# A hybrid decoder trunk: two first weight loads on another queue, later outputs and norms in the differential heads, other places in the tile before the last, roots one group behind, two output jobs begun

## The chip, the cores and the metric

The kernel runs on one core of a Trainium2 chip, as one program. The metric is the device time of one execution in microseconds (us). Before the change the median of three runs is 1193.19 us (1192.76 to 1195.35).

The engines are written as in the profile: PE (TensorE, matmuls), DVE (VectorE), ACT (ScalarE), POOL (GpSimd) and SP (SyncE, which here only issues DMAs). Each has its own queue and takes its instructions in a fixed order.

## The reference

The reference is a two-layer decoder trunk over 512 tokens of width 1024, in float32:

```
h = x
h += W_out [ dilated_mixture(qa, ka, va) | rms(differential(qb, kb, vb)) ]   # q, k, v from one projection of rms(h)
h += W_down( gelu(g) * v ),  [g | v] = conv3( W_up rms(h) )
h += W_out( rg_lru(conv4(xr)) * gelu(gate) ),  [gate | xr] = W_in rms(h)     # layer 1
h += W_down( gelu(g) * v )                                                   # second feed-forward
```

Differential attention takes two softmaxes per head and subtracts lam times the second from the first; its output is normalised once more per head (`b_sub_norm`). The recurrent unit has r = sigmoid(block matmul), i = sigmoid(block matmul), a = exp(-8 r softplus(-a_param)), and scans h = a h + sqrt(1 - a^2) (i x).

## The kernel before, in words

Activations lie transposed, channels on the partitions and the 512 tokens along the free axis. Every matmul of the projections is three products of halves (`mm3`): each float32 operand is split into a high part (`wh`, `xh`) and the remainder (`wl`, `xl`). For a weight unit SP loads the raw block, ACT casts it to `wh` (L104) and DVE subtracts to `wl` (L106); units are fetched two ahead.

**Attention.** Eight tiles run in a row: four differential heads (the B tiles, n = 0 to 3), then four pairs of dilated heads (the A tiles, n = 4 to 7). Each tile has 16 groups of six projection matmuls (L348 to L350, output `pj`). The list `line` holds the 128 groups and, behind them, the first matmuls of the output projection (`early_out`, output `mm`, three matmuls a piece). Everything else of a tile is put between groups of `line` by `place(g, f)`, with `g` from the table that `where(n)` returns, counted in groups from the start of the tile, so that 27.3 falls among the next tile's groups. The table's keys: `qk` the transposes of q and k (`qkt`, L414), `sc` the scores with their softmax in three batches (`S`, L447; 128 and 256 columns, then 384, then 512), `tr` the transposes of the probabilities (`pt`, L468, called pt1 to pt4 here, each followed by the cast `pth` on ACT, L471, and the remainder `ptl` on DVE, L472), `out` the product with v (`O`, L482 to L484), and `norm` for the B tiles (`norm`). PE keeps the order in which the code is written; for ACT and DVE a scheduler fixes the order when the program is built.

In a B tile `out` also copies O to `ob` (L571), squares it to `obsq` (L573) and splits the squares in `obh` (ACT, L126) and `obl` (DVE, L127); `norm` begins with two matmuls that sum them over the partitions (`obms`, L129 with `obh`, L130 with `obl`). The softmax of a row block is one DVE instruction that adds the bias and takes the maximum (L458), an exponential on ACT (L461) and a scaling (L556, or L515 in an A tile).

**The start.** `first_tile` issues, all on SP, the two halves of the first block of x and of the first weight unit in turn (L306, L307), then three more pairs. ACT casts the halves of the weight unit (L323).

**The recurrent layer.** For eight blocks of 128 channels `lru_in` projects and convolves (`us` L704, `cv` L706 on ACT and three taps on DVE, L708) and splits (`xrh` L820, `xrl` L822); `lru_gates` runs the gates' matmuls two blocks later (`pr`, `pi`) and three functions on ACT (L837 to L839). `lru_decay` takes four blocks at a time: four exponentials (L849) and squares, and directly behind them four square roots (L857). Functions of ACT belong to tables; going from one table to another costs an ACT_TABLE_LOAD. `after(f)` chains these parts on ACT in the order of the calls. At the end `gelu` makes `gh` and `gl` (L897, L899), and `out_proj` runs eight jobs of 24 matmuls, each over k = 0 to 7.

Of the kernel before, what the change touches and what calls it, by code (L numbers as in the profile page):

```python
# [12 lines left out]
F32 = mybir.dt.float32  # L13
# [6 lines left out]
P = 128  # L20
S = 512
D = 1024
KC = D // P
# [4 lines left out]
NT = 8  # L28
# [2 lines left out]


BATCHES = ((0, 1), (2,), (3,))
PLACES = dict(qk=9, sc=(12, 14, 16), tr=(18.5, 20.7, 23.5, 25.2), step=1, out=27.3, norm=29)
LAST = dict(qk=7.5, sc=(9.8, 10.5, 11.2), tr=(12.7, 13.4, 14.2, 15), step=0.35, out=16.2, norm=18)

OUT_GROUP = 0.65
# [25 lines left out]
def trunk(  # L63
# [15 lines left out]
    nc = tc.nc  # L79
# [14 lines left out]
    def nm(s):  # L94
        uid[0] += 1
        return f"{s}{uid[0]}"
# [22 lines left out]
    def mm3(out, wh, wl, xh, xl, first, last, order=lambda ins: ins):  # L119
        order(T.matmul(out, wh, xh, start=first, stop=False))  # L120
        order(T.matmul(out, wh, xl, start=False, stop=False))  # L121
        return order(T.matmul(out, wl, xh, start=False, stop=last))  # L122
# [96 lines left out]
    with ExitStack() as actx:  # L219
# [78 lines left out]
        def first_tile():  # L298


            xr = [ap2.tile([P, 13 * P], F32, tag=("pth", "ptl")[u % 2], name=nm("xr"))[:, : 2 * S] for u in range(4)]
            wr = [rawp.tile([P, 2 * CW], F32, tag="raw", name=nm("raw")) for u in range(4)]
            for u in range(4):
                for j in range(2 if u == 0 else 1):
                    cx, cw = (slice(j * S, (j + 1) * S), slice(j * CW, (j + 1) * CW)) if u == 0 else (slice(None),) * 2
                    nc.sync.dma_start(xr[u][:, cx], xT[u][:, cx])  # L306
                    nc.sync.dma_start(wr[u][:, cw], w_att[ORDER[0], u][:, cw])  # L307
            nc.sync.dma_start(pt[:, KC:], par[:, KC:])
            units = []
            for u in range(4):  # L310
                if u:
                    x_split(xr[u], (2 * u, 2 * u + 1))
                    units.append(split(wr[u], 2 * CW))
                    with tc.issue_after(last.ins):
                        x_square(xr[u - 1], (2 * u - 2, 2 * u - 1))
                    continue
                wh = whp.tile([P, 2 * CW], F32R, tag="wh", name=nm("wh"))
                wl = wlp.tile([P, 2 * CW], F32R, tag="wl", name=nm("wl"))
                for j in range(2):
                    cw = slice(j * CW, (j + 1) * CW)  # L320
                    last = x_split(xr[0], (j,))
                    with tc.issue_after(last.ins):
                        last = A.copy(wh[:, cw], wr[0][:, cw])  # L323
                    V.tensor_tensor(wl[:, cw], wr[0][:, cw], wh[:, cw].bitcast(F32), ALU.subtract)
                units.append((wh, wl))
            x_square(xr[3], (6, 7))
            return units
# [94 lines left out]
        oT = {}  # L422

        def where(n):
            return LAST if n == NT - 1 else PLACES

        def head_bias(h):
            bt = ap2.tile([P, S], F32, tag="bias", name=nm("bias"))
# [113 lines left out]
        def attn_b(n):  # L542

            p = ORDER[n]
            st = {}

            def sc(blocks):
                if blocks[0] == 0:
                    st["b"] = head_bias(4 + p)
                rows = products(tiles[n]["qk"], blocks)  # L550
                for i in blocks:
                    for c in range(2):
                        st[i, c] = softmax_row(rows[c, i], i, st["b"])
                        if c == 0:
                            e0, r0 = st[i, 0]
                            A.activation(e0, e0, AF.Copy, scale=r0)  # L556
                        else:
                            (e0, _), (e1, r1) = st[i, 0], st[i, 1]
                            V.tensor_tensor(r1, r1, lam, ALU.mult)
                            V.scalar_tensor_tensor(e0, e1, r1, e0, ALU.mult, ALU.add)  # L560

            def tr(i):
                if i == 0:
                    st["pt"] = pt_tiles()
                transposed(st[i, 0][0], i, *st["pt"])

            def out():
                o_ps = bank("O")
                pv(o_ps, tiles[n]["v"], *st["pt"])
                st["o"] = smp.tile([P, S], F32, tag="sq", name=nm("ob"))  # L570
                A.copy(st["o"], o_ps)  # L571
                sq = smp.tile([P, S], F32, tag="sm3", name=nm("obsq"))
                A.activation(sq, o_ps, AF.Square)  # L573
                hi = smp.tile([P, S], F32R, tag="sq", name=nm("obh"))
                lo = smp.tile([P, S], F32R, tag="t", name=nm("obl"), bufs=1)
                st["ms"] = mean_rows("obms", hi, sq, lo)

            def norm():
                o = st["o"]
                ps, products_of = st["ms"]  # L580
                products_of(pe)
                y = smp.tile([P, S], F32, tag="sm3", name=nm("oby"))
                A.activation(y, ps, AF.Ln, bias=epsb)
                A.activation(y, y, AF.Exp, scale=-0.5)
                t = smp.tile([P, S], F32, tag="sq", name=nm("obt"))
                V.tensor_tensor(t, y, y, ALU.mult)
                V.scalar_tensor_tensor(t, ps, EPS, t, ALU.add, ALU.mult)
                V.tensor_scalar(t, t, -0.5 * (1.0 - LAM_INIT), 1.5 * (1.0 - LAM_INIT), ALU.mult, ALU.add)
                V.tensor_tensor(y, y, t, ALU.mult)
                V.scalar_tensor_tensor(o, o, col(C_BS), y, ALU.mult, ALU.mult)  # L590
                hi, lo = o_tiles(p)
                A.copy(hi, o)
                V.tensor_tensor(lo, o, hi.bitcast(F32), ALU.subtract)

            at = where(n)
            steps = [(g, partial(sc, b)) for g, b in zip(at["sc"], BATCHES)]
            steps += [(g, partial(tr, i)) for i, g in enumerate(at["tr"])]
            return steps + [(at["out"], out), (at["norm"], norm)]


# [111 lines left out]
    def ffn(l, nxt, last):  # L712
# [37 lines left out]
        down(1, a1)  # L750
        down(2, a2)

    def out_proj(xs, resid, nxt, order=range(KC), begun=()):
        for m in range(KC):
            if m < len(begun):
                ps, (wh, wl) = begun[m]
                k = order[-1]
                c = slice(k * P, (k + 1) * P)
                mm3(ps, wh[:, c], wl[:, c], *xs[k], False, True)
            else:  # L760
                ps = job(xs, order)
            V.tensor_tensor(h[m], ps, resid(m), ALU.add)
            norm_chunk(m, nxt)
# [43 lines left out]
    def after(f):  # L807

        with ExitStack() as st:
            if mark[0] is not None:  # L810
                st.enter_context(tc.issue_after(mark[0].ins))
            mark[0] = f()
# [31 lines left out]
    def lru_decay(ns):  # L844

        def decay():
            for n in ns:

                last = A.activation(rr[n], rr[n], AF.Exp, scale=spm8[:, n : n + 1])  # L849
                a2 = tmp.tile([P, S], F32, tag="sq", name=nm("a2"), bufs=2)  # L850
                A.activation(a2, rr[n], AF.Square)
                V.scalar_tensor_tensor(tt[n], a2, 1.0, tt[n], ALU.add, ALU.mult)
            return last

        def root():
            for n in ns:
                last = A.activation(tt[n], tt[n], AF.Sqrt, bias=tinyb)  # L857
            return last

        after(decay)  # L860
        after(root)

    def lru_scan(n):
        V.tensor_tensor(uu[n], uu[n], tt[n], ALU.mult)
        V.tensor_tensor_scan(uu[n], rr[n], uu[n], 0.0, ALU.mult, ALU.add)  # L865

    def gate_in(n):
        ps = job(xs)
        g = gg[n] = actp.tile([P, S], F32, tag=f"ah{n}", name=nm("gate"))
        V.tensor_tensor(g, ps, state["rs"], ALU.mult)  # L870

    ins = []
    for n in range(KC):
        ins.append(lru_in(n))
        if n > 1:
            lru_gates(n - 2, *ins[n - 2])
        if n == KC // 2 + 1:
            lru_decay(range(KC // 2))
        if n > KC // 2 + 1:
            lru_scan(n - KC // 2 - 2)  # L880
    for n in range(2):
        gate_in(n)
        lru_gates(KC - 2 + n, *ins[KC - 2 + n])
        lru_scan(KC // 2 - 2 + n)
    lru_decay(range(KC // 2, KC))
    for n in range(2, KC):
        gate_in(n)
        if n < 6:
            lru_scan(KC // 2 + n - 2)
    hg = []  # L890

    def gelu():
# [8 lines left out]
        return last  # L901

    after(gelu)
    out_proj(hg, lambda m: h[m], C_FFN_G[1])
    ffn(1, None, True)


# [69 lines left out]
```

## Time and profile before

| what | value |
|---|---|
| median of the runs | 1193.19 us (1192.76 to 1195.35) |
| profiled execution, its own time | 1195.96 us |
| its span | 1194.1 us |
| PE busy | 1181.2 us (99%), 5566 matmuls |
| DVE busy | 811.4 us (68%) |
| ACT busy | 585.6 us (49%) |
| SP queue, data moved | 113.24 MB, 29.8% of 16 DMA engines |
| granted TensorE clock | 1.00 |

The span runs from the first to the last recorded instruction; 1.86 us of the execution's own time lie outside it. A row of a timeline gives the start in the span, the busy time, the engine, the line, the operation and the tiles, and in brackets how long the engine had been idle and what it had waited for. ACTq and SPq rows are instructions that issue a DMA.

### The profile page before, as it was taken

To read this page: it belongs to the slowest core of one execution; us is meant where nothing else is said; L and a number is where in the kernel's file an instruction comes from. 1 tells how busy PE (TensorE), PEld (TensorE's weight loads), DVE (VectorE), ACT (ScalarE), POOL (GpSimd) and SP (SyncE) were. 2 spreads that over 40 slices of the span, in tenths; PEclk is the share of its full clock that TensorE was granted. 3 is DMA by queue.
4 is the path that set the end of the run, shared out by engine and by line. 5 is a ranking of instruction groups with operands and counts; after the bars stand their busy time and mean duration, and the time that the engine had idled before them with its cause. 6 is when DMAs were issued, how large, how long until landed. Compare 5 with 4: busy or idle time off the path is not lost.

```text
span 1194.1 us, 14625 instructions
## 1 busy us (share of the span) xinstructions
PE 1181.2 (99%) x5566; PEld 990.6 (83%) x5566; DVE 811.4 (68%) x1327; ACT 585.6 (49%) x951; POOL 0.7 (0%) x6
## 2 busy tenths in 40 slices
PE   8999999999999999999999999999999999999998
PEld 8988888788888888888888878888888888888887
DVE  6977888688777763577436888668777763677431
ACT  6667788765444432344225688454444441444220
POOL 0000000000000000000000000000000000000000
PEclk9999999999999999999999999999999999999999
DMA  7221222062323232323233313323232323333221
GB/s 255 68 79 54 67 67 71 19 211 89 106 89 106 89 106 88 106 89 106 88 106 102 111 36 124 106 89 102 92 101 94 100 94 95 100 95 100 92 85 54
DMA packets 33910, 114.31 MB, mean 96 GB/s; under 512 B 3888, under 2 KB 4656, under 8 KB 33840
## 3 DMA queue, kind: packets, MB, share of 16 engines
q1 hardware_dynamic: 33552, 113.24, 29.8%
q8 instruction: 44, 0.72, 0.3%
q14 instruction: 26, 0.21, 0.1%
q10 hardware_dynamic: 288, 0.14, 0.0%
HBM read 111.27 MB, written 2.10 MB: 95 GB/s over the span
## 4 chain that ended last, share of the span: by engine, by line
PE 83%; ACT 3%; DVE 2%; issue 0%; DVEq 0%
PE mm L120 26%; PE mm L121 26%; PE mm L122 26%; ACT sm L461 1%; PE pj L348 1%; PE pj L350 1%; PE pj L349 1%; PE pt L468 1%; ACT sm L515 1%; PE S L447 0%; PE O L489 0%; DVE u L865 0%; DVE sm L458 0%; PE qkt L414 0%; DVE cv L708 0%
## 5 line engine op out<-in xcount | busy, mean ns | idle before, releaser
L104 ACT CAST wh<-raw 128x1024 fp32r<-128x1024 f32 (+1 forms) x207 | 211.1, 1021 | 285.8 <-PE mm L121 256.8
L122 PE MATMUL mm<-xh,wl 128*128 128x512 f32 x896 | 348.6, 389 | 0.0
L121 PE MATMUL mm<-xl,wh 128*128 128x512 f32 x896 | 348.6, 389 | 0.0
L120 PE MATMUL mm<-xh,wh 128*128 128x512 f32 x896 | 348.6, 389 | 0.0
L106 DVE TENSOR_TENSOR wl<-raw,wh 128x1024 fp32r<-128x1024 f32 (+1 forms) x207 | 244.8, 1184 | 43.0 <-ACT wh L104 39.4
L120 PEld LDWEIGHTS mm<-xh,wh 128*128 128x128 f32 x896 | 168.2, 188 | 35.0
L121 PEld LDWEIGHTS mm<-xl,wh 128*128 128x128 f32 x896 | 168.2, 188 | 35.0
L122 PEld LDWEIGHTS mm<-xh,wl 128*128 128x128 f32 x896 | 168.2, 188 | 34.9
L708 DVE SCALAR_TENSOR_TENSOR cv<-us,pt,cv 128x511 f32<-128x511 f32 (+2 forms) x216 | 160.5, 747 | 3.5
L120 PE MATMUL mm<-fh,wh 128*128 128x512 f32 x384 | 149.4, 389 | 0.0
L121 PE MATMUL mm<-fl,wh 128*128 128x512 f32 x384 | 149.4, 389 | 0.0
L122 PE MATMUL mm<-fh,wl 128*128 128x512 f32 x384 | 149.4, 389 | 0.0
L704 DVE TENSOR_TENSOR us<-mm,rs 128x512 f32<-128x512 f32 x104 | 71.6, 688 | 93.9 <-PE mm L122 93.6
L740 DVE TENSOR_TENSOR h<-mm,h 128x512 f32<-128x512 f32 (+1 forms) x49 | 33.2, 680 | 141.4 <-PE mm L122 141.4
L348 PE MATMUL pj<-wh,xh 128*128 128x384 f32 x256 | 92.7, 362 | 2.5 <-ACT wh L323 2.5
L729 ACT CAST fh<-cv 128x512 fp32r<-128x512 f32 x48 | 29.8, 621 | 126.4 <-DVE cv L726 126.4
L350 PE MATMUL pj<-wl,xh 128*128 128x384 f32 x256 | 87.2, 341 | 0.0
L349 PE MATMUL pj<-wh,xl 128*128 128x384 f32 x256 | 87.2, 341 | 0.0
L706 ACT ACTIVATE cv<-us,pt 128x512 f32<-128x512 f32 x104 | 84.3, 813 | 0.9 <-DVE us L704 0.6
L120 PEld LDWEIGHTS mm<-fh,wh 128*128 128x128 f32 x384 | 72.1, 188 | 15.0
L122 PEld LDWEIGHTS mm<-fh,wl 128*128 128x128 f32 x384 | 72.1, 188 | 15.0
L121 PEld LDWEIGHTS mm<-fl,wh 128*128 128x128 f32 x384 | 72.1, 188 | 14.9
(202 smaller groups left out, 1238.6 us busy)
## 6 DMA issues: line engine op xcount, KB each, us to landing
raw<-in_w_up_dram SPq DMA_DIRECT2D x96, 512.0 KB, 3.5
raw<-in_w_dn_dram SPq DMA_DIRECT2D x48, 512.0 KB, 3.5
raw<-in_w_att_dram SPq DMA_DIRECT2D x31, 384.0 KB, 3.4
raw<-in_w_ri_dram SPq DMA_DIRECT2D x16, 512.0 KB, 3.5
raw<-in_w_ao_dram SPq DMA_DIRECT2D x8, 512.0 KB, 3.6
raw<-in_w_ro_dram SPq DMA_DIRECT2D x8, 512.0 KB, 3.5
raw<-in_xT_dram SPq DMA_DIRECT2D x4, 512.0 KB, 4.4
out_dram<-h SPq DMA_DIRECT2D x7, 256.0 KB, 2.0
```

What stands on the lines that cost most here:

```text
L104: A.copy(hi, src)
L106: V.tensor_tensor(lo, src, hi.bitcast(F32), ALU.subtract)
L120: order(T.matmul(out, wh, xh, start=first, stop=False))
L121: order(T.matmul(out, wh, xl, start=False, stop=False))
L122: return order(T.matmul(out, wl, xh, start=False, stop=last))
L348: pe(T.matmul(o, xs[k][0][:, tb], wh[:, cw], start=k == 0, stop=False))
L349: pe(T.matmul(o, xs[k][1][:, tb], wh[:, cw], start=False, stop=False))
L350: pe(T.matmul(o, xs[k][0][:, tb], wl[:, cw], start=False, stop=k == KC - 1))
L704: V.tensor_tensor(u, ps, state["rs"], ALU.mult)
L706: A.activation(c, u, AF.Identity, scale=col(wcol + (taps - 1) * stride), bias=col(bcol))
L708: V.scalar_tensor_tensor(c[:, d:], u[:, : S - d], col(wcol + (taps - 1 - d) * stride), c[:, d:], ALU.mult, ALU.add)
L740: V.tensor_tensor(h[m][:, t], ps[:, t], h[m][:, t], ALU.add)
```

## The change

Five edits, none of which changes what is computed:

1. The two halves of the first weight unit are issued by ACT instead of SP.
2. The one table of places becomes three. B tiles put `out` and `norm` later (27.3 to 28.3, 29 to 30.2) and pt4 at 25.4 instead of 25.2, which is still behind the same group. Tile n = 6 gets a table of its own.
3. `oby` of the norm takes the buffer `t` instead of `sm3`.
4. The four roots leave `lru_decay` and become `lru_root`, called one block later.
5. `out_proj` of layer 1 begins two jobs over k = 0 to 6 and finishes them with k = 7; the matmuls are the same ones in another order.

```diff
-PLACES = dict(qk=9, sc=(12, 14, 16), tr=(18.5, 20.7, 23.5, 25.2), step=1, out=27.3, norm=29)
+PLACES_B = dict(qk=9, sc=(12, 14, 16), tr=(18.5, 20.7, 23.5, 25.4), out=28.3, norm=30.2)
+PLACES_A = dict(qk=9, sc=(12, 14, 16), tr=(18.5, 20.7, 23.5, 25.2), step=1, out=27.3)
+LAST_BUT_ONE = dict(qk=9, sc=(12, 14, 15.8), tr=(18.2, 20.2, 22.6, 24.4), step=0.9, out=26.4)
...
-                    nc.sync.dma_start(wr[u][:, cw], w_att[ORDER[0], u][:, cw])
+                    (nc.sync if u else A).dma_start(wr[u][:, cw], w_att[ORDER[0], u][:, cw])
...
-            return LAST if n == NT - 1 else PLACES
+            return {NT - 1: LAST, NT - 2: LAST_BUT_ONE}.get(n, PLACES_A if ORDER[n] < 4 else PLACES_B)
...
-                y = smp.tile([P, S], F32, tag="sm3", name=nm("oby"))
+                y = smp.tile([P, S], F32, tag="t", name=nm("oby"), bufs=1)
...
+    def begin(xs):
+
+        wh, wl = next_unit()
+        ps = mm.tile([P, S], F32, tag="mm", name=nm("mm"))
+        for k in range(KC - 1):
+            c = slice(k * P, (k + 1) * P)
+            mm3(ps, wh[:, c], wl[:, c], *xs[k], k == 0, False, tc.keep_in_program_order)
+        return ps, (wh, wl)
...
+        after(decay)
+
+    def lru_root(ns):
+
         def root():
             for n in ns:
                 last = A.activation(tt[n], tt[n], AF.Sqrt, bias=tinyb)
             return last
 
-        after(decay)
         after(root)
...
-        if n == KC // 2 + 1:
-            lru_decay(range(KC // 2))
-        if n > KC // 2 + 1:
-            lru_scan(n - KC // 2 - 2)
+        if n == half + 1:
+            lru_decay(range(half))
+        if n == half + 2:
+            lru_root(range(half))
+        if n > half + 1:
+            lru_scan(n - half - 2)
...
-    out_proj(hg, lambda m: h[m], C_FFN_G[1])
+    out_proj(hg, lambda m: h[m], C_FFN_G[1], begun=[begin(hg) for _ in range(2)])
```

What this makes of the queues is seen in the built program. Line numbers after the change are two higher up to the norm, and more behind it (L849 becomes L860, L857 becomes L872).

At the start, SP's queue before holds the halves of x (`xr_129`) and of the weight unit (`raw_133`) in turn:

```order
L306 DMA xr_129<-in_xT_dram 128x512
L307 DMA raw_133<-in_w_att_dram 128x384
L306 DMA xr_129<-in_xT_dram 128x512
L307 DMA raw_133<-in_w_att_dram 128x384
L306 DMA xr_130<-in_xT_dram 128x1024
L307 DMA raw_134<-in_w_att_dram 128x768
```

After, ACT's queue begins with these rows:

```order
L158 ACT_TABLE_LOAD
L162 DMA pt<-in_par_dram 128x8
L309 DMA raw_133<-in_w_att_dram 128x384 x2
L233 ACTIVATE xh_150<-xr_129,pt 128x512
L325 CAST wh_148<-raw_133 128x384
L233 ACTIVATE xh_156<-xr_129,pt 128x512
L325 CAST wh_148<-raw_133 128x384
L233 ACTIVATE xh_162<-xr_130,pt 128x512
L233 ACTIVATE xh_166<-xr_130,pt 128x512
L106 CAST wh_170<-raw_134 128x768
L242 ACTIVATE xsq_174<-xr_129 128x512
```

The two weight halves stand on ACT behind a small load of parameters, and the square of the first block of x (`xsq_174`) has moved behind the cast of the second weight unit.

In the B tiles, ACT before takes O of one tile (`ob_849`, `obsq_851`, `obh_853`) ahead of the next tile's softmax (`sm_880`, `sm_887`: 128 columns; `sm_895`: 256):

```order
L571 COPY ob_849<-O_836 128x512
L573 ACTIVATE obsq_851<-O_836 128x512
L104 CAST wh_1039<-raw_1037 128x768
L126 CAST obh_853<-obsq_851 128x512
L461 ACTIVATE sm_880,sum_883<-sm_880,mx_881 128x128
L461 ACTIVATE sm_887,sum_890<-sm_887,mx_888 128x128
L366 COPY qkraw_922<-pj_706 128x256
L378 ACTIVATE v_923<-pj_706,rstd 128x128
L556 ACTIVATE sm_880<-sm_880,sum_883 128x128
L461 ACTIVATE sm_895,sum_898<-sm_895,mx_896 128x256
```

After, the same O (`ob_901`, `obsq_903`, `obh_905`) stands behind the softmax of both batches, and `obh` behind a copy of q and k and of v as well:

```order
L106 CAST wh_1039<-raw_1037 128x768
L463 ACTIVATE sm_858,sum_861<-sm_858,mx_859 128x128
L463 ACTIVATE sm_865,sum_868<-sm_865,mx_866 128x128
L558 ACTIVATE sm_858<-sm_858,sum_861 128x128
L463 ACTIVATE sm_873,sum_876<-sm_873,mx_874 128x256
L463 ACTIVATE sm_880,sum_883<-sm_880,mx_881 128x256
L558 ACTIVATE sm_873<-sm_873,sum_876 128x256
L573 COPY ob_901<-O_888 128x512
L575 ACTIVATE obsq_903<-O_888 128x512
L368 COPY qkraw_922<-pj_706 128x256
L380 ACTIVATE v_923<-pj_706,rstd 128x128
L128 CAST obh_905<-obsq_903 128x512
```

On PE the matmuls stand in these places. Before: pt4, 12 group matmuls, O, 6, S of 128 and 256, 6, the norm's two, 6, S of 384, 12, S of 512. After: pt4, 18 group matmuls, S of 128 and 256, O, 12, S of 384, the norm's two, 12, S of 512.

In the recurrent layer, ACT before runs the last exponential of the first four blocks (`r_6393`), the roots (`t_...` with `tinyb`), and then the convolution of block 6 (`cv_6453`) and the gates of block 4 (`r_6470`, `u_6471`):

```order
L849 ACTIVATE r_6393<-r_6393,spm_466 128x512
L857 ACT_TABLE_LOAD
L857 ACTIVATE t_6224<-t_6224,tinyb 128x512
L851 ACTIVATE a_6413<-r_6393 128x512
L857 ACTIVATE t_6281<-t_6281,tinyb 128x512
L857 ACTIVATE t_6338<-t_6338,tinyb 128x512
L857 ACTIVATE t_6395<-t_6395,tinyb 128x512
L706 ACTIVATE cv_6453<-us_6451,pt 128x512
L837 ACT_TABLE_LOAD
L837 ACTIVATE r_6470<-pr_6462,pt 128x512
L838 ACTIVATE u_6471<-pi_6463,pt 128x512
L839 ACTIVATE t_6472<-r_6470,sp_464 128x512
```

After, block 6's convolution (`cv_6449`) and block 4's gates (`r_6466`, `u_6467`) go ahead of the roots, with a table load more:

```order
L860 ACTIVATE r_6393<-r_6393,spm_466 128x512
L708 ACTIVATE cv_6449<-us_6447,pt 128x512
L862 ACTIVATE a_6413<-r_6393 128x512
L848 ACT_TABLE_LOAD
L848 ACTIVATE r_6466<-pr_6458,pt 128x512
L849 ACTIVATE u_6467<-pi_6459,pt 128x512
L831 CAST xrh_6454<-cv_6449 128x512
L850 ACTIVATE t_6468<-r_6466,sp_464 128x512
L872 ACT_TABLE_LOAD
L872 ACTIVATE t_6224<-t_6224,tinyb 128x512
L872 ACTIVATE t_6281<-t_6281,tinyb 128x512
L872 ACTIVATE t_6338<-t_6338,tinyb 128x512
```

The roots now stand behind the split of block 6 (`xrh_6454`), and two table loads stand where one was between the exponentials and the roots.

## Rows read from the trace of the kernel before

**Rows 1.** The page's first part: busy time of each engine, share, instructions.

```profile
PE 1181.2 (99%) x5566; PEld 990.6 (83%) x5566; DVE 811.4 (68%) x1327; ACT 585.6 (49%) x951; POOL 0.7 (0%) x6
```

**Rows 2.** What PE waited for, whole span: us in total, times, longest us.

```profile
PE O L483 <- DVE ptl L472: 2.6, 3, 1.0
...
PE pt L468 <- DVE o L531: 1.1, 2, 0.8
PE pt L468 <- DVE ptl L472: 1.0, 2, 0.8
PE pr L121 <- DVE xrl L822: 0.7, 1, 0.7
```

**Rows 3.** Timeline of 0.7 to 2.6 us: start, us, queue, line, DMA issued.

```profile
0.77 0.39 ACTq L160 DMA_DIRECT2D pt<-in_par_dram  x1
...
2.12 0.43 SPq L307 DMA_DIRECT2D raw<-in_w_att_dram  x1
```

**Rows 4.** Timeline of 5.9 to 14.0 us, first weight unit.

```profile
8.39 0.51 ACT L323 CAST wh<-raw 128x384 fp32r<-128x384 f32 x1 [2.23 <-DMA raw<-in_w_att_dram]
...
8.95 0.69 PE L348 MATMUL pj<-wh,xh 128*128 128x384 f32 x1 [2.32 <-ACT wh L323]
...
11.78 0.96 DVE L106 TENSOR_TENSOR wl<-raw,wh 128x768 fp32r<-128x768 f32 x1
...
12.96 0.52 PE L348 MATMUL pj<-wh,xh 128*128 128x384 f32 x1
...
13.75 0.34 PE L348 MATMUL pj<-wh,xh 128*128 128x384 f32 x1
```

**Rows 5.** Timeline of 84 to 113 us, PE, second B tile.

```profile
88.33 0.50 PE L483 MATMUL O<-ptl,v 128*128 128x512 f32 x1 [0.95 <-DVE ptl L472]
...
89.95 0.27 PE L484 MATMUL O<-pth,v 128*128 128x128 f32 x1
91.27 0.33 PE L447 MATMUL S<-qh,qh 64*128 64x128 f32 x2
...
93.31 0.40 PE L129 MATMUL obms<-obh,ones_r 128*128 128x512 f32 x1
```

**Rows 6.** Timeline of 90 to 97.5 us, ACT and DVE, the same tile.

```profile
91.96 0.63 ACT L126 CAST obh<-obsq 128x512 fp32r<-128x512 f32 x1
...
92.98 0.68 DVE L127 TENSOR_TENSOR obl<-obsq,obh 128x512 fp32r<-128x512 f32 x1
...
93.91 0.40 ACT L461 ACTIVATE sm<-sm,mx 128x128 f32<-128x128 f32 x1 [1.32 <-DVE mx L458]
...
94.69 0.35 ACT L366 COPY qkraw<-pj 128x256 f32<-128x256 f32 x1
...
95.21 0.40 ACT L556 ACTIVATE sm<-sm,sum 128x128 f32<-128x128 f32 x1
...
95.50 0.50 ACT L461 ACTIVATE sm<-sm,mx 128x256 f32<-128x256 f32 x1
```

**Rows 7.** Timeline of 209 to 229 us, tiles n = 6 and 7.

```profile
210.44 0.81 DVE L472 TENSOR_TENSOR ptl<-pt,pth 128x128 fp32r<-128x128 f32 x3
...
215.68 0.33 PE L447 MATMUL S<-qh,qh 64*128 64x128 f32 x2
```

**Rows 8.** Timeline of 699 to 714 us, recurrent layer.

```profile
699.11 0.69 DVE L704 TENSOR_TENSOR us<-mm,rs 128x512 f32<-128x512 f32 x1
...
705.59 0.80 ACT L706 ACTIVATE cv<-us,pt 128x512 f32<-128x512 f32 x1
...
706.41 1.28 ACT L837 ACT_TABLE_LOAD   x1
707.70 0.69 ACT L837 ACTIVATE r<-pr,pt 128x512 f32<-128x512 f32 x1
```

**Rows 9.** Timeline of 757 to 760 us, the last split ahead of the output projection.

```profile
758.55 0.69 DVE L899 TENSOR_TENSOR gl<-u,gh 128x512 fp32r<-128x512 f32 x1 [0.69 <-ACT gh L897]
...
759.39 0.40 PE L121 MATMUL mm<-gl,wh 128*128 128x512 f32 x1
```

More of the change, by code (lines that the diff above doesn't have):

```diff
@@ L758, in out_proj @@
                 c = slice(k * P, (k + 1) * P)
-                mm3(ps, wh[:, c], wl[:, c], *xs[k], False, True)
+                mm3(ps, wh[:, c], wl[:, c], *xs[k], False, True, tc.keep_in_program_order)
             else:
@@ L870, in gate_in @@
         V.tensor_tensor(g, ps, state["rs"], ALU.mult)
+    half = KC // 2
     ins = []
@@ L883, in trunk @@
         lru_gates(KC - 2 + n, *ins[KC - 2 + n])
-        lru_scan(KC // 2 - 2 + n)
-    lru_decay(range(KC // 2, KC))
+        lru_scan(half - 2 + n)
+    lru_decay(range(half, KC))
     for n in range(2, KC):
         gate_in(n)
+        if n == 2:
+            lru_root(range(half, KC))
         if n < 6:
-            lru_scan(KC // 2 + n - 2)
+            lru_scan(half + n - 2)
     hg = []
```

## The prediction

> **What bounds the kernel now.** I read the busy shares first. PE works 1181.2 us of the span of 1194.1 [rows 1], so only what PE executes, or what keeps PE waiting, can move the time. No edit changes a matmul, so the question is PE's waits. The table of PE's waits [rows 2] is the second view: next to the start it has only O waiting for the remainder of the probabilities (three times, 2.6 us), transposes waiting for `ptl` (1.0) and `o` (1.1), and one gate matmul (0.7). A wait costs PE some 0.17 us more than its idle time, because the next matmul would have started before the one ahead ended: O's second matmul begins at 88.33 after 0.95 idle [rows 5] and is 1.1 late. With that, O's three waits are worth 3.1 us, the three short ones in tiles 6 and 7 about 1.8, the one of 0.8 ahead of them 0.9, and the gates' 1.2 with a short one on `xrh`. Timelines are the third view; they show who is late, and why.
>
> The profiled execution took 1195.96 us, 2.77 over the median of the runs. I make the sum against it and put the difference on the median, which supposes that the runs wait in the same places.
>
> **The start.** PE has done the first half unit and then stands idle 2.32 us, until 8.95, since ACT's cast of the second half waited for its load until 8.39 [rows 4]. That load was issued at 2.12 on SP [rows 3] and took 6.3 us. After the change it is ACT's third DMA. ACT's first is issued at 0.77 and holds its queue 0.39 us [rows 3]; two more at that rate put the second half at about 1.6, half a us earlier, and off the queue in which the large blocks follow. If it lands as soon as the rest of the chain allows, PE goes on at about 6.5: at most 2.4 us gained. At least nothing, if it lands as late as before. A second brake is the clock: matmuls of 384 columns last 0.52 us up to 12.96 and 0.34 from 13.75 on [rows 4], PE's lower and upper level of 1.2 and 2.4 GHz in their length, while the column of the granted clock reads 1.00. If the change to the upper level stays at its time, the head start is spent at half speed and about half of it is lost. The next unit is no obstacle: its `wl` is ready at 12.7 [rows 4], and ACT no longer squares x ahead of its cast, which takes 0.5 off. I take -1.8, nearer to the full gain, because the load that comes late is the only late one.
>
> The rule against this is in the Trainium skill, "DMA: Bandwidth & Descriptors", section "Issuing engines are not separate DMA queues": DMAs run on the same 16 engines whoever issues them, and a second issuer saves only the time to initiate. By that rule the start gains about 0.5, and the sum below would be 1.3 higher; no row of this trace has two busy issuers to decide it.
>
> **The B tiles, out and norm one group later.** O now comes after 18 group matmuls and the first scores, 2 us later, and `ptl` is there: its three waits, 3.1 us, go. Two breaks between groups and other matmuls go as well. I put 0.1 to 0.15 to a break, an estimate from groups of six with and without one beside them: 0.2 to 0.3 a tile. The question is what is late next. It is the norm. On ACT `obh` stood ahead of the softmax; now it stands behind both batches of it. Let T be the first score matmul of a tile, 91.27 in rows 5. Its exponential follows 2.64 later, at 93.91 [rows 6], with `obl` (0.60 to the next start) between on DVE; without `obl` there, it starts at T+2.04. An instruction of ACT starts about 0.1 before its predecessor ends: two exponentials of 128 columns with their sums take 0.78 to the copy at 94.69, copy and `v` together 0.52 to 95.21, a scaling 0.29 to 95.50 [rows 6]; an exponential of 256 columns about 0.5, its scaling about 0.4, `ob` and `obsq` about 0.5 each like `obh`. So `ob` starts at 2.04 + 0.78 + 0.29 + 2 x 0.5 + 0.4 = T+4.5, and `obh` at 4.5 + 1.0 + 0.5 = T+6.0, ends at 6.6, and `obl` ends at T+7.3 (0.63 and 0.68, rows 6).
>
> PE is earlier. From T it runs scores and one group in 2.04 (91.27 to 93.31, rows 5), one more group (1.04), O (88.33 to the end of its last matmul, and the one ahead: about 1.95) and the scores of 384 columns (0.75, as many columns as the first two batches): it wants `obh` at T+5.75 and `obl` at T+5.95. It waits for `obl` about 1.4 us in all. Before, `obl` came (92.98 + 0.68) just in time for 93.71. So each of the first three B tiles loses 1.4 and gains the breaks: tile 0, whose O never waited, is 1.1 slower; tiles 1 and 2 come out even (-0.1 each).
>
> In the fourth B tile the next tile is an A tile, and the built order puts more ahead of `obh`: one more scaling of 128 (0.3), one of 256 (0.4), a second copy pair (0.5), a squaring (0.5), and the first exponential of 384 columns (0.6). By the same steps `obh` starts at T+8.3 and `obl` ends at T+9.7: PE waits 3.7. Less O's 0.8 and the breaks this is 2.6 slower. The pause is time for DVE, so the transpose that waited 0.8 (the longest in rows 2; 0.9 lost) in the next tile waits no more. Sum for the B tiles: 1.1 - 0.2 + 2.6 - 0.9 = +2.6. Bounds: if ACT got to `obh` in time everywhere, -3.1 - 0.9 - 1.0 = -5.0; if each walk is 0.5 short, +4.6.
>
> The buffer of `oby` costs nothing: `obl`, which shares it, is read by the matmul that `oby` waits for anyway.
>
> **Tile n = 6.** The projection tail's three waits are worth 1.8. The new table asks for the third pair of transposes three output matmuls (0.7) and a stall earlier. Its wait was for `ptl` of the first transposes, which DVE began at 210.44 [rows 7] behind the scaling of q and k; that chain comes about 0.6 later, as ACT now runs the second exponential of 384 columns and its scaling ahead of the last copies. I get the first score of the last tile at 217.3 in place of 215.68 [rows 7], and, as the softmax chain from there to the second pt2 is 0.6 shorter, +1.0 at its end. Bounds: -1.8 (all three waits gone) and +2.5 (the chain not shortened, another wait for the same ACT).
>
> **Roots.** `us` of block 6 is ready at 699.8, but ACT comes to its `cv` only at 705.59, behind a table load and the four roots [rows 8]; that makes the gate matmul late. After the change `cv` goes ahead of those, 4.3 us earlier (1.28 for the load, four roots and a square at about 0.6), and the wait of 1.2 goes. One table load more is added to ACT, 1.28 with the next function directly behind it [rows 8]. It lies beside PE's work: block 7's split moves 0.6 later, and was done more than a us before PE asked for it, of which 0.4 is left once PE is 1.2 earlier. I take -1.2; bounds -1.2 and +0.5.
>
> The Trainium skill, "ScalarE: Activation LUTs", section "What ACT_TABLE_LOAD costs", speaks against this edit: a switch costs a drain as well, 2.66 us together. With that, two loads ahead of block 7's split would make it 2.8 late, and the sum 2.4 higher; rows 8 have the next function 1.29 after the load's start, so the trace does not agree.
>
> **Begun jobs.** The last `gl` ends at 759.24 and PE reads it at 759.39 [rows 9]: no loss now, hence nothing to gain: 0, between -0.1 and +0.3.
>
> **Sum.** -1.8 + 2.6 + 1.0 - 1.2 + 0 = +0.6: 1196.6 for a profiled execution, 1193.8 for the median.
>
> **Rivals.** (1) The norms find their splits in time: their waits stay under 0.4 each. For it: ACT is busy under half of the span, and its instructions may run ahead where I queued them. Against: its order is fixed, and the softmax ahead of `obh` needs DVE's answers. Then the B tiles give -5.0 + 4 x 0.3 = -3.8, and the sum is -5.8: 1187.4. If tile 6 succeeds too, 1184.6. (2) The start gives only the issue time, all else as forecast: +1.9, 1195.1. For it: bytes ahead of the second half are the same. Against: the late load is one out of many. (3) Slower: the norm's wait is longer than walked. If the cast of the next weight unit, which heads ACT's list ahead of the softmax and waits for PE's last group, and the bias maximum behind it slip by 0.5, every norm waits 0.5 more, +2.0 over four tiles, and with tile 6's upper end (+1.5) the sum is +4.1: 1197.3. It decides from a wait of 1.9 on in the first three tiles. Against: nothing new is queued ahead of that cast.
>
> **How the numbers follow.** Within 0.2% (2.4 us, about what a measurement of this kernel can tell from no change) lies 1190.8 to 1195.6. The forecast has 0.42, with an own range of 1191.5 to 1196; rival 1 has 0.24, rival 2 0.19, rival 3 0.15. Faster: rival 1 and 0.05 from the forecast's lower end, 0.29. Slower: rival 3, and 0.08 from the upper ends of the forecast and of rival 2, 0.23. Same: 0.48. The range for 8 in 10 reaches from rival 1 to rival 3: 1186.5 to 1197.5.
>
> **What would show it.** Each step has its row: PE's idle time ahead of its second weight half under 0.5 us; no wait of O for `ptl`; waits of the norm's matmuls for `obh` or `obl` of about 1.4 three times and 3.7 once; a wait of pt3 for `ptl` of 1 us or more near 210; none of the gates for `xrl`. I am wrong if the norm's waits sum to under 3 us, or if the start still idles 2 us.

## The result and the profile after

| | before | after |
|---|---|---|
| median of runs, us | 1193.63 (4 runs, 1192.76 to 1195.35) | 1200.99 (4 runs, 1199.80 to 1202.75) |
| profiled execution, us | 1195.96 | 1200.73 |
| its span, us | 1194.1 | 1198.6 |

The ratio is 1.0061, 95% interval 1.0044 to 1.0078: 7.4 us slower, outside of the predicted range. Line numbers of after are two higher than before's from the tables of places on, and 11 to 19 higher behind `begin`.

The page of after, its first part: busy time of each engine, share of the span and instructions.

```profile
PE 1181.4 (99%) x5566; PEld 992.9 (83%) x5566; DVE 813.3 (68%) x1327; ACT 588.2 (49%) x952; POOL 0.7 (0%) x6
```

PE works as long as before [rows 1], so the time has gone into its pauses. The view of PE's waits in after, whole span (us in total, times, longest):

```profile
PE obms L131 <- ACT obh L128: 5.2, 4, 3.1
PE pj L350 <- ACT wh L325: 2.6, 2, 1.7
PE pt L470 <- DVE o L533: 1.5, 1, 1.5
...
PE obms L132 <- DVE obl L129: 0.9, 4, 0.2
PE S L449 <- DVE mx L460: 0.6, 1, 0.6
PE pt L470 <- DVE ptl L474: 0.6, 1, 0.6
```

Against [rows 2], O's three waits and the gate's have gone, and the norm's have come, 6.1 us in two rows. I compared the start of the same instruction in the two traces, mark by mark:

| mark on PE | before, us | after, us | lead (-) or lag so far | this stretch |
|---|---|---|---|---|
| first score of tile 0 | 41.69 | 41.30 | -0.39 | -0.39 |
| 512-column scores of tile 4 (behind the fourth norm) | 149.49 | 153.53 | +4.04 | +4.43 |
| first score of tile 5 | 168.71 | 171.65 | +2.94 | -1.10 |
| first norm behind the attention | 267.66 | 272.51 | +4.85 | +1.91 |
| third norm behind the attention (recurrent layer done) | 803.39 | 806.86 | +3.47 | -1.38 |
| end of PE's last matmul | 1190.32 | 1193.79 | +3.47 | 0 |
| end of the span | 1194.07 | 1198.57 | +4.50 | +1.03 |

From the first of these marks on, two traces of the same program agree to 0.1 us (before and after were each traced twice); only the start scatters, by some 2 us (first score of tile 0 at 39.74 to 41.83 in eight traces with before's start, at 40.32 to 42.66 in five with the new one). For the start the medians of runs are therefore used, for all else the traces.

The norm first. Timeline of after, 90 to 96 us, ACT, DVE and PE in the second B tile, whose first score matmul starts at T = 88.68 (start, us, engine, line, operation, idle time before it and its releaser):

```profile
90.68 0.40 ACT L463 ACTIVATE sm<-sm,mx 128x128 f32<-128x128 f32 x1 [1.24 <-DVE mx L460]
...
93.15 0.57 ACT L573 COPY ob<-O 128x512 f32<-128x512 f32 x1
...
94.62 0.61 ACT L128 CAST obh<-obsq 128x512 fp32r<-128x512 f32 x1
95.26 0.69 DVE L129 TENSOR_TENSOR obl<-obsq,obh 128x512 fp32r<-128x512 f32 x1 [0.16 <-ACT obh L128]
95.28 0.49 PE L131 MATMUL obms<-obh,ones_r 128*128 128x512 f32 x1 [0.69 <-ACT obh L128]
...
96.01 0.50 PE L132 MATMUL obms<-obl,ones_r 128*128 128x512 f32 x1 [0.23 <-DVE obl L129]
```

In [rows 6] `obh` stood 1.95 ahead of the tile's first exponential; now it stands 3.94 behind it, and PE idles 0.69 and 0.23. In the fourth B tile the pause is longer, and it has a second price. PE of after, 145 to 154 us:

```profile
145.31 0.34 PE L449 MATMUL S<-ql,qh 64*128 64x384 f32 x2
148.74 0.50 PE L131 MATMUL obms<-obh,ones_r 128*128 128x512 f32 x1 [3.09 <-ACT obh L128]
149.47 0.80 PE L132 MATMUL obms<-obl,ones_r 128*128 128x512 f32 x1 [0.22 <-DVE obl L129]
150.06 0.53 PE L350 MATMUL pj<-wh,xh 128*128 128x384 f32 x1
...
152.92 0.33 PE L350 MATMUL pj<-wh,xh 128*128 128x384 f32 x1
...
153.53 0.50 PE L449 MATMUL S<-qh,qh 64*128 64x512 f32 x2
```

The same in the view by windows (window, length, then busy time of PE, PEld, DVE, ACT, POOL, granted clock, DMA share, GB/s):

```profile
146.00:149.00 3.00, 0.26 (x1) 0.19 (x1) 2.29 (x9) 3.00 (x9) 0.00 (x0) 1.00 0.00 0
149.00:152.00 3.00, 2.78 (x9) 2.44 (x9) 0.50 (x2) 1.99 (x5) 0.00 (x0) 0.58 0.02 5
152.00:155.00 3.00, 3.00 (x16) 2.34 (x15) 1.72 (x4) 2.52 (x7) 0.00 (x0) 0.85 0.00 0
```

Behind the 3.09 us pause the granted clock is 0.58, PE's lower level of 1.2 GHz: matmuls of 384 columns last 0.53 until about 152.9 and 0.33 after that. From the norm's first matmul to the next scores PE takes 4.79 us. In the second B tile, where the granted clock is 1.00 and PE waits as long for `obl` (0.23), the same matmuls take 3.25 (95.28 to 98.53), and behind the third norm 3.24. So the lower clock costs some 1.55 us, beside the pause itself.

### The profile page after: what moved, and what is told of

It is laid out like the page before. It is cut to its first block, busy times and chain, and to the rows that moved or that the text cites. A ratio compares the mean times of both kernels' runs of the same rounds, so it can differ in the third digit from the quotient of the medians.

```text
span 1198.6 us, 14612 instructions
## 1 busy us (share of the span) xinstructions
PE 1181.4 (99%) x5566; PEld 992.9 (83%) x5566; DVE 813.3 (68%) x1327; ACT 588.2 (49%) x952; POOL 0.7 (0%) x6
## 4 chain that ended last, share of the span: by engine, by line
PE 94%; ACT 4%; DVE 1%; DMA 1%; issue 0%; ACTq 0%; DVEq 0%
PE mm L124 26%; PE mm L122 26%; PE mm L123 26%; PE pj L350 4%; PE pj L351 3%; PE pj L352 3%; ACT sm L463 1%; PE pt L470 1%; PE S L449 1%; ACT sm L517 1%; PE qkt L416 1%; DMA raw<-in_w_att_dram 1%; PE O L491 0%; ACT wh L106 0%; DVE wl L108 0%
## 5 line engine op out<-in xcount | busy, mean ns | idle before, releaser
L742 DVE TENSOR_TENSOR h<-mm,h 128x512 f32<-128x512 f32 (+1 forms) x49 | 33.2, 680 | 141.4 <-PE mm L124 141.4
```

The lines of the kernel that those rows point to most:

```text
L742: V.tensor_tensor(h[m][:, t], ps[:, t], h[m][:, t], ALU.add)
```

## The experiments

Medians stand, with the number of runs, against those of the kernel before on the same chip; brackets are 95% intervals of the ratio.

**The start alone** (start_only).

```
-                    nc.sync.dma_start(wr[u][:, cw], w_att[ORDER[0], u][:, cw])
+                    (nc.sync if u else A).dma_start(wr[u][:, cw], w_att[ORDER[0], u][:, cw])
```

> The kernel before with the first edit alone (both halves of the first weight unit issued by ACT). Theory A (the profile's account of the changed kernel is the whole account, and the start is worth what its trace shows): the first stamp of per-token sums comes about 0.4 us earlier than in the kernel before, the second half of the weight unit still lands near 8 us, and the time is within 1 us of before. Theory B (the timed runs of before start better than its one profiled execution, and the edit loses about 2.5 us there): 1.5 to 3 us slower than before.

Measured: 1196.07 (10 runs) against 1194.07 (31), ratio 1.0017 [1.0008, 1.0026]: 2.0 us slower, where I had forecast 1.8 gained, as theory B has it. In the traces the first score of tile 0 comes 0.8 later on average (five with the edit, eight with before's start); the 2.0 is that of the medians. Its start, PE and the DMA queues, 0.7 to 8 us:

```profile
0.73 1.34 SPq L306 DMA_DIRECT2D xr<-in_xT_dram  x3
1.19 0.93 ACTq L307 DMA_DIRECT2D raw<-in_w_att_dram  x2
...
5.40 0.51 ACT L323 CAST wh<-raw 128x384 fp32r<-128x384 f32 x1 [0.54 <-DMA raw<-in_w_att_dram]
5.96 0.69 PE L348 MATMUL pj<-wh,xh 128*128 128x384 f32 x1 [1.10 <-ACT wh L323]
...
7.18 0.51 ACT L323 CAST wh<-raw 128x384 fp32r<-128x384 f32 x1 [0.64 <-DMA raw<-in_w_att_dram]
7.74 0.69 PE L348 MATMUL pj<-wh,xh 128*128 128x384 f32 x1 [0.45 <-ACT wh L323]
```

**The kernel before once more** (before_again), unchanged, for the scatter of its start.

> The kernel before, unchanged, for a second trace. Theory A: the same PE stamps within 0.5 us from the first scores on and an end behind PE of 3.7 to 4.8 us, so that the profiled 1195.96 was an execution at the upper end of the runs. Theory B: the second weight half lands 2 us earlier than in the first trace, and all stamps are 2 us earlier.

Measured: 1194.17 (10), ratio 0.9999. Its start:

```profile
1.65 0.42 SPq L306 DMA_DIRECT2D xr<-in_xT_dram  x1
2.11 0.43 SPq L307 DMA_DIRECT2D raw<-in_w_att_dram  x1
2.59 0.43 SPq L306 DMA_DIRECT2D xr<-in_xT_dram  x1
...
4.60 0.49 ACT L323 CAST wh<-raw 128x384 fp32r<-128x384 f32 x1
...
5.14 0.44 PE L348 MATMUL pj<-wh,xh 128*128 128x384 f32 x1 [0.28 <-ACT wh L323]
...
6.73 0.72 ACT L231 ACTIVATE xh<-xr,pt 128x512 fp32r<-128x512 f32 x1 [1.64 <-DMA xr<-in_xT_dram]
...
7.36 0.49 ACT L323 CAST wh<-raw 128x384 fp32r<-128x384 f32 x1
7.91 0.44 PE L348 MATMUL pj<-wh,xh 128*128 128x384 f32 x1 [1.47 <-ACT wh L323]
```

Neither theory holds whole: from the first scores on this trace is 1.3 us ahead of the first one of before. Here the first weight half is cast at 4.60, in start_only at 5.40: the edit delays it. And the second half, in [rows 4] the late load on which I built, lands 1.2 us earlier, at 7.21 in place of 8.37, and 1.3 ahead of the second block of x (512 KB, issued at 2.59). Nor is it the only late load: ACT waits until 6.73 for the second half of the first x block. With the edit SP has two DMAs less ahead of the second block and issues it at 1.65, and the second weight half landed 0.2 to 1.2 us behind it in each of the five traces with the edit (in start_only at 7.16, the block at 6.79).

**The start edit with the first x block in four pieces** (start_split), so that SP issues the second block at 2.6 again.

```
-                    nc.sync.dma_start(xr[u][:, cx], xT[u][:, cx])
+                    for c0 in (cx.start, cx.start + S // 2) if u == 0 else (None,):
+                        cq = cx if c0 is None else slice(c0, c0 + S // 2)
+                        nc.sync.dma_start(xr[u][:, cq], xT[u][:, cq])
```

> The kernel before with the first edit, and with the two halves of the first block of x issued as four DMAs of 256 columns on SP, so that the second block of x is issued at about 2.6 us as before and not at 1.65. Theory A (the edit loses because the second block, 512 KB, is issued ahead of the second weight half and shares the DMA engines with it): the second half lands at 6.5 us or earlier, PE begins it by 7.1, and the time is that of before within 1 us, 2 us under the edit alone. Rival (a load issued on ACT's queue is slower by itself): it lands behind 7.2 us, and the time stays 1.5 to 2.5 us above before.

Measured: 1193.67 (11) against 1193.88 (27), 0.9999 [0.9990, 1.0008]; the second half lands at 5.95, 1.7 ahead of the block (issued at 2.59). PE begins it at 7.55 and not by 7.1, because ACT comes to its cast only behind the second half of x (6.38). The loss has gone, so the issue by ACT is not what costs; what is left is the earlier block. The later first half is not it: it is cast at 5.43 here too. That the four smaller loads of x do something besides was not tested. A gain is not seen either, with an interval of -1.2 to +1.0 us.

**Out and norm of the B tiles alone** (out_norm_only: the tables and the buffer of `oby`).

```
-PLACES = dict(qk=9, sc=(12, 14, 16), tr=(18.5, 20.7, 23.5, 25.2), step=1, out=27.3, norm=29)
+PLACES_B = dict(qk=9, sc=(12, 14, 16), tr=(18.5, 20.7, 23.5, 25.4), out=28.3, norm=30.2)
+PLACES_A = dict(qk=9, sc=(12, 14, 16), tr=(18.5, 20.7, 23.5, 25.2), step=1, out=27.3)
...
-            return LAST if n == NT - 1 else PLACES
+            return LAST if n == NT - 1 else PLACES_A if ORDER[n] < 4 else PLACES_B
...
-                y = smp.tile([P, S], F32, tag="sm3", name=nm("oby"))
+                y = smp.tile([P, S], F32, tag="t", name=nm("oby"), bufs=1)
```

> The kernel before with out at 28.3 and norm at 30.2 in the B tiles and the other buffer for oby, tile n = 6 and all else as before. Theory A (norm waits, and a lower clock behind the long one): PE waits 1.3 to 1.4 us at each of the first three norms and 3.7 at the fourth, the granted clock falls for some 3.5 us behind the fourth, and the time is 3.3 us above before. Rival (the norm waits only take the place of O's, no clock): +1.7 us.

Measured: 1196.89 (10), 1.0024 [1.0014, 1.0033], +2.8; +3.37 between the marks, with the norm's waits of 5.2 and 0.9 as in after, and a granted clock of 0.57 from 149 to 152. That is theory A.

**After with the norm 1 and 3 places later** (after_norm_31 and after_norm_33).

```
-PLACES_B = dict(qk=9, sc=(12, 14, 16), tr=(18.5, 20.7, 23.5, 25.4), out=28.3, norm=30.2)
+PLACES_B = dict(qk=9, sc=(12, 14, 16), tr=(18.5, 20.7, 23.5, 25.4), out=28.3, norm=31.2)
```

(33.2 in place of 31.2 in the second.)

> The changed kernel with norm at 31.2, one group behind the scores of 384 columns. It parts the fourth tile from the other three. Theory A: the first three norms wait 0.3 us at most; the fourth still waits 3 us or more, as another copy pair comes ahead of its split, and the granted clock falls behind it; 1200.99 less 3 x 1.2 gives 1197 to 1198. Rival (the fall of the clock belongs to the sum of the waits, not to the long one): no fall, 1195 or less.

> The changed kernel with norm at 33.2 in place of 30.2, so that the norm's matmuls stand one group behind the scores of 512 columns; all else as changed. Theory A (the norm's waits and the lower clock behind the fourth make most of the loss): no wait of the norm's matmuls, no fall of the clock near 150, some 8 us faster than the changed kernel, 1192 to 1193.5. Rival (the loss lies in the start and in what comes behind the attention): 3 us faster at most, 1197 or more.

Measured: with 31.2, 1195.81 (10) against 1193.88; with 33.2, 1192.97 (10) against 1194.07, 0.9992 [0.9983, 1.0001]. Relative to before that is +1.9 and -1.1, where after is +7.4. PE's waits for the norm with 31.2:

```profile
PE obms L131 <- ACT obh L128: 2.4, 1, 2.4
```

The first three have gone, the fourth is left, with a granted clock of 0.71 and 0.73 from 146 to 152; I had expected 3 us or more of it, and the time is over 1 us below what I had expected. With 33.2 there is no wait of the norm, the clock stays at 1.00, the B tiles take 3.25 less than in before, and one new wait is next, a transpose for `ptl` (1.6 near 152). So the pauses of the norm are what the B tiles lost, and the later O is worth having once the norm follows late enough.

**The table of tile n = 6 alone** (lbo_only).

```
+LAST_BUT_ONE = dict(qk=9, sc=(12, 14, 15.8), tr=(18.2, 20.2, 22.6, 24.4), step=0.9, out=26.4)
...
-            return LAST if n == NT - 1 else PLACES
+            return {NT - 1: LAST, NT - 2: LAST_BUT_ONE}.get(n, PLACES)
```

> The kernel before with the table of tile n = 6 alone. Theory A (as in the trace of the changed kernel: a wait of the scores of 512 columns for the maximum of those of 384, a longer wait of pt3 and of the second pt2): waits of 0.6, 0.6 and 1.5 us in that order, the first norm behind the attention 1.9 us later by the trace, 1.9 slower. Rival (the waits come from the later arrival of the tile, behind the norm's waits): the three waits of before, within 0.5 us of before.

Measured: 1197.35 (9) against 1193.88 (27), 1.0024 [1.0015, 1.0034], with three runs near 1195.4 and six near 1197.5. The trace is of an execution of the upper group (1197.34). In it the three waits are 0.6, 0.6 and 1.5, as theory A has them, the tile costs 1.8, and the last store lands later (below), by 1.2; the time is 1.6 us above what I had expected. What parts the two groups of runs is not settled.

**Roots alone** (root_only: `lru_root` one block later, without the begun jobs).

```
-    out_proj(hg, lambda m: h[m], C_FFN_G[1], begun=[begin(hg) for _ in range(2)])
+    out_proj(hg, lambda m: h[m], C_FFN_G[1], begun=())
```

(taken from after, with its tables, its start and the buffer of `oby` put back too)

> The kernel before with the roots one block later alone; the output jobs of the recurrent layer run whole, as before. Theory A (the begun jobs are what lets the roots' gain through: the last split of the gelu part comes at a time that PE's head start does not move): the gates' wait of 1.2 us goes, a new wait of 0.7 and 0.5 us at the last k of the first output job takes its place, and the time is within 0.5 us of before. Rival (the roots gain by themselves, as forecast): 1.2 us faster.

Measured: 1194.02 (11) against 1193.84 (15), 1.0006 [0.9997, 1.0014]. The gate's wait has gone, and PE is 1.27 earlier up to 758 us. There it waits for the last split, in PE's timeline of root_only:

```profile
757.66 0.39 PE L122 MATMUL mm<-gh,wl 128*128 128x512 f32 x1
758.54 0.50 PE L120 MATMUL mm<-gh,wh 128*128 128x512 f32 x1 [0.50 <-ACT gh L914]
759.27 0.50 PE L121 MATMUL mm<-gl,wh 128*128 128x512 f32 x1 [0.23 <-DVE gl L916]
```

What was won is given back: at 761.90 PE is level with before (761.91). In [rows 9] that split was just in time; an earlier PE makes it late.

**Combinations**, all with before's start and before's table for tile n = 6: later out and norm at 33.2 with the roots, without the begun jobs; then with them; then with the fourth B tile's norm at 39.2 besides (best, best_begun and best_b39).

> The kernel before with the parts that gain by the traces: out at 28.3 and norm at 33.2 in the B tiles with the other buffer for oby, and the roots one block later; the start, tile n = 6 and the output jobs as before. Theory A (the parts add up: -3.2 for the B tiles, -1.3 for the roots): 4.5 us faster than before, 1189 to 1190.5, no wait of O, of the norms or of the gates. Rival (the wait of a transpose for ptl in the first A tile, 1.8 us in the trace with the norm at 33.2, grows, or the gain of the B tiles belongs to the other start): 2.5 us or less.

> The kernel with out at 28.3, norm at 33.2 and the later roots, to which the two begun output jobs are added. Theory A: the wait of 1.2 us at the last k of the first output job goes, 1.2 us faster than without the begun jobs, 1189.1, 4.8 under before. Rival (the begun jobs cost by themselves, two jobs' results coming late together): no gain over 1190.3.

> The same with the norm of the fourth differential head at 39.2 instead of 33.2, so that DVE makes the remainders of the first transposes of the next tile ahead of the norm's arithmetic. Theory A: the wait of the third transposes for them (1.8 us in the traces with norm at 33.2) falls by 0.6, what two instructions of the norm took ahead of them; 1188.5. Rival (the remainders wait for the scaling of q and k anyway): no change, 1189.1.

Measured: 1190.32 (6) against 1193.88, 0.9967 [0.9955, 0.9978]; 1189.67 (5) against 1193.84, 0.9966 [0.9954, 0.9979]; 1188.52 (5) against 1193.84, 0.9954 [0.9941, 0.9968]. The first gains 3.6 where I had expected 4.5: the gates' wait has gone, but it has the same wait for `gh` and `gl` as root_only (0.5 and 0.2, near 754), and the roots give nothing; with the begun jobs it is gone and 1.35 of the roots is kept. The third is 5.3 us faster than before, the fastest median here. PE's waits in it:

```profile
PE pj L351 <- ACT wh L326: 1.2, 2, 1.0
PE O L494 <- DVE ptl L475: 1.1, 1, 1.1
...
PE pt L471 <- DVE o L534: 1.0, 2, 0.8
PE pt L471 <- DVE ptl L475: 0.2, 1, 0.2
```

The transpose's 1.6 has become a wait of O of 1.1, and from the first score of tile 0 to that of tile 5 the trace takes 0.9 us less than the second's. The difference of the medians to the second (1.2 us) lies inside of their intervals.

**After once more** (after_again), unchanged.

> The changed kernel, unchanged, for a second trace and more runs; it asks where the 1 us lies by which its time stands above the sum of its parts (2.0 for the start, 3.3 for the B tiles, 1.8 for tile n = 6, -1.3 for the roots with the begun jobs: 5.8). Theory A (the last store landed late by chance in the first trace): the second trace ends 3.7 us behind PE, and the median of more runs is nearer to 5.8 above before, 1199.5 to 1200. Theory B (the late last store belongs to this program): it ends 4.7 us behind PE again, and the time stays at 1201.

Measured: 1200.74 (5) against 1192.82 (9), 1.0058 [1.0044, 1.0071]; the same marks from tile 0 on, to 0.1 us. The DMAs issued after 1188 us, in after (queue, KB, us from issue to landing):

```profile
out_dram<-h SPq DMA_DIRECT2D x1, 128.0 KB, 1.7
out_dram<-h ACTq DMA_DIRECT2D x1, 128.0 KB, 2.8
```

In before they take 1.7 and 1.8. In this second profile of after the last store again takes 2.8 us, and the span ends 4.74 behind PE (theory B); in lbo_only it takes 3.0. The two kernels with the norm moved later have the same table for tile 6, and end their span 3.74 and 3.75 behind PE, as before does. So the late store comes back with the program. Why is open.

## Why the prediction was wrong, step by step

The forecast was +0.6; measured are +7.4 and, in the repeat, +7.9 between the medians (+6.9 by the ratio). The parts sum to +6.8: start +2.0, B tiles +3.3, tile 6 +1.9, roots with begun jobs -1.4, last store +1.0. What the medians show beyond that was found in no place of the traces. The largest miss is the start, 3.8 us; each other part missed by 1.0 us or less.

- **The bound** was right: PE's busy time did not move, its waits did.
- **The start** (-1.8, measured +2.0) is the step that failed. That the late load "is the only late one" was read from one execution. In the second trace of before it lands 1.2 us earlier, and in seven traces with the same start 0.6 to 2.0 earlier: I took scatter for a property of the order, and took the gain off a median whose executions, by these traces, have less of that wait. I priced ACT's issue of the load and not what SP issues in the room that it leaves: of a moved DMA the queue that it leaves has to be walked as well. The lower bound of no gain was therefore no bound. PE idles 1.70 us ahead of its second half in after and 2.68 in the repeat, where I forecast under 0.5. In place of the gain the runs showed the second half landing behind SP's 512 KB block, and a loss of 2.0 that goes once that block is issued at 2.59 again. Rival 2 came from the Trainium skill, "DMA: Bandwidth & Descriptors", section "Issuing engines are not separate DMA queues"; its first half, that the loads share their engines whoever issues them, agrees with the second half landing behind SP's block. That the second issuer only saves is not what was measured in start_only, and the half microsecond of rival 2 is too small for start_split to tell from none (-1.2 to +1.0 us).
- **B tiles** (+2.6, measured +3.3: tile 0 +1.0, tiles 1 and 2 -0.25 each, tile 3 +4.0, the transposes' wait -1.1). The walk along ACT held: T+2.04, 4.5, 6.0 and 7.3 for the starts of the exponential, `ob` and `obh` and the end of `obl` became 2.00, 4.47, 5.94 and 7.27 in the rows above. The waits walked as 1.4 and 3.7 were 0.7 and 3.1 for `obh`, 0.2 each for `obl`, and with the matmul that would have started before its predecessor ended, some 1.3 and 3.65. O's waits went. The mis-sized term is the fourth tile, +2.6: it left out that PE resumes at 1.2 GHz, 1.55 us, and measured +4.0. I had read both levels at the start [rows 4] and did not apply them to a pause that I had just forecast.
- **Tile n = 6** (+1.0, measured +1.9; lbo_only +1.8) had the right sign and too small a size. The new rows of PE in after are these:

```profile
204.72 0.49 PE L449 MATMUL S<-qh,qh 64*128 64x512 f32 x1 [0.57 <-DVE mx L460]
...
214.41 0.55 PE L470 MATMUL pt<-ident,sm 128*128 128x128 f32 x3 [0.56 <-DVE ptl L474]
...
232.45 0.44 PE L470 MATMUL pt<-ident,sm 128*128 128x128 f32 x2 [1.47 <-DVE o L533]
```

  The second I had named as 1 us or more; it is 0.56. The first, the largest scores waiting for a maximum of the batch ahead, I had not foreseen, and the last, 1.5 in place of 1.1 in two [rows 2], I had put as a chain 0.6 shorter.
- **Roots and begun jobs** (-1.2 and 0, measured -1.4 together). The total is right by luck, since the split is wrong: root_only gives nothing, the begun jobs alone were not run, and the two together keep the gain. By my own rows `gl` is 0.15 ahead of PE; from this I had the begun jobs gain nothing, and did not carry PE's 1.2 earlier into that step. The Trainium skill, "ScalarE: Activation LUTs", section "What ACT_TABLE_LOAD costs", would have made the added table load 2.66 us. The trace does not agree, and it decides: ACT in after has the next function 1.30 behind the load's start, and the gate's wait gone:

```profile
711.08 1.28 ACT L872 ACT_TABLE_LOAD   x1
712.38 2.56 ACT L872 ACTIVATE t<-t,tinyb 128x512 f32<-128x512 f32 x4
```

- **The last store** (+1.0) stood in no step.
- **The rivals.** Rival 1 did not come: PE idled 0.9 us at each of the first three norms and 3.3 at the fourth, not under 0.4. Rival 3 named the right side, with the norm's wait as mechanism; but the waits were the walked ones, not 0.5 longer, and its price of 1197.3 is 3.7 short. It took the start's gain of 1.8 for certain.

## What to carry to other kernels

When a DMA is moved to another queue, walk the queue that it leaves too: what comes forward there competes with it, and one execution's late load says nothing before a second one shows it. When a step moves one place later (O), the work on its result (`ob`, `obsq` and `obh` on ACT) moves as well and lands behind other work; what reads that result (the norm) has to move as far as that work does. Here 3 more places made +3.3 into -3.2. Price a forecast pause of PE at the clock that follows it, not by its length alone. Two edits on one chain are priced in sequence: a wait that goes uncovers the next, and an edit that is worth nothing alone may be what keeps the gain.

## What the runs showed of the hardware

- Behind a pause of 3.1 us before the norm the granted clock was 0.58 (149 to 152 us in after), and with one of 2.4 us, which ended at 147.2, it was 0.71 and 0.73 (146 to 152 us in after_norm_31); the pauses of 0.7 in the other B tiles, and one of 1.6 in the first combination, left it at 1.00. At the lower level matmuls of 384 columns lasted 0.53 us, at the upper 0.33.
- Across two issuing queues a small load (second weight half) landed behind a block of 512 KB issued at nearly the same time (1.67 and 1.65) on the other, by 0.2 to 1.2 us, and 1.7 ahead of it when issued 0.9 us earlier (start_split).
- Executions with the same start differ in their first 42 us by 2.1 (eight) and 2.3 us (five), and hardly at all afterwards.
- The last store of the same size and queue lands after 1.7 to 1.8 us in ten programs, and after 2.8 to 3.0 in two, in one of them in both traces.
